# Elementwise work of a decoder layer's mixer, rebuilt: which engine does which step, and on how many columns

## The chip, the core and the metric

One core of a Trainium2 chip runs the whole kernel. The metric is device time in microseconds: three timed runs, of which the median counts. TensorE does the matmuls, VectorE (DVE), ScalarE (ACT) and GpSimd (POOL) the elementwise work, SyncE (SP) issues most DMAs. Each engine takes its instructions strictly in the order in which the kernel emits them, and waits for another engine by semaphores.

## What is computed

One inference step of one decoder layer, in float32, for 256 prompt tokens and 8 sample sequences of 8 tokens (320 columns; features lie on the partitions). Two head groups share one input projection:

```python
p = x @ w_in                                   # 2048 -> 5408
xc = causal_conv(u_x); r, i = sigmoid(xc @ wa + ba), sigmoid(xc @ wx + bx)
a = exp(-8 * r * softplus(-lam)); h_t = a_t * h_(t-1) + sqrt(1 - a*a) * (i * xc)     # RG-LRU, 8 blocks of 128
y_lru = h * gelu(u_gate)
z = u + (prev - u) * mu                        # RWKV-7: token shift of r, k, v and of three code tiles
w = exp(-exp(-0.5) * sigmoid(w0 + tanh(wd) @ w_up)); a = sigmoid(a0 + ad @ a_up); g = sigmoid(gd) @ g_up
kk = k * k_k; kk = kk / sqrt(max(sum(kk * kk), 1e-24)); k = k * (1 + (a - 1) * k_a)
S_t = S * w - (S kk) (kk * a)^T + v k^T; o_t = S_t r                                 # 16 heads of 64
y_rwkv = (group_norm(o) * ln_w + ln_b + sum(r * k * r_k) * v) * g
x = LN(ALPHA * x + [y_lru, y_rwkv] @ w_out); then cross-attention with its norm, then a squared-ReLU MLP with its norm
```

## The kernel before

**The main line** is a stream of 512 KB pieces of weights (`Stream`, lines 236 to 285). A piece is loaded on SyncE's queue, ScalarE rounds it to a first float32r part `wh`, and `Stream.poll` has the rest `wl = wraw - wh` made by VectorE or GpSimd. `mm_piece` (line 366) then runs three matmuls for each block of 128 x 128: `wh` with the two parts of the activations, and `wl` with the first. A feature tile of 128 rows and 320 columns takes 16 such blocks.

**The order** is made when the program is built. `Sched` (lines 108 to 208) keeps an estimated clock and an estimated free time of each engine (`account`), and side tasks are generators that it resumes between the stream's matmuls once their next step should be ready. `tt` (line 308) lets the engine with the earlier estimated end, VectorE or GpSimd, do a product or a sum of two tiles; `copy` chooses likewise between VectorE and ScalarE. Nothing of this is decided on the chip.

**The stages.** `w_in` (86 pieces) runs from the start to 516 us of the profile and `wk` (32 pieces, the memory keys, 256 columns) to 665 us; the mixer's side tasks run in these two, and `sch.drain()` at the end of `wk` finishes them. After it come `wv`, `w_out` with a layer norm, `wq`, attention, `wo` with a norm, and the MLP. `on_win` (line 1001) takes each finished tile of `w_in`: code tiles, then for each of 8 pairs of heads r, k, v, then x and gate of one LRU block.

**The side tasks** of the mixer, with the names that matter:

- `shifted` (539): ScalarE copies the tile from PSUM in two pieces, the difference to the token before is made by `tt`, then VectorE adds it in two `scalar_tensor_tensor` steps (256 columns, and 64 in sequences of 8). `sh_out` is kept by two GpSimd copies.
- `rwkv` (606): decays and keys; the norm of the keys is a matmul with the block of ones `bones` and a reciprocal over 320 columns; `BK` and `AR` (scaled b and k, a and r) are made in halves; their products inside the chunks become `GM`; then the sequence of four prompt chunks (729 to 763), where a chunk multiplies the state `S`, the inverse `XT` and the updates `UV`; at last the group norm, whose two sums are float32r matmuls of two parts of the tile (`halves`, `head_sums`) with a reciprocal over 320 columns.
- `invert` (797): the triangular inverses of the chunks. The products go to DRAM and back so that forty 16 x 16 blocks lie one to a partition (`Mp`, `Xp`); 30 dependent VectorE steps of 15 to 64 elements solve them (820 to 827); SyncE stores the result (828) and reads it back (833); then two levels of block products.
- `sample` (880): the 8 sample sequences as one more chunk.
- `lru_task` (934): convolution, the two gates (one as 1 / (1 + exp), the other as tanh of half), a scan, and the gate by tanh.

All matmuls of the side tasks but `head_sums` are plain float32, which the profile shows as two records each. An instruction that the planner accounts has line 230 (the wrapper), so groups are told apart by tiles. In a matmul's names the moving operand stands before the weights.

Of the kernel before, what the change touches and what calls it, by code (L numbers as in the profile page):

```python
# [9 lines left out]
F32 = mybir.dt.float32  # L10
F32R = mybir.dt.float32r
# [20 lines left out]
T_CODE = [24, 25, 26]                    # shift-tile numbers of the low-rank codes  # L32
WIN_TILES = []                           # (kind, index)
# [21 lines left out]
# constant block: identity, ones per 64-block, ones, room, masks  # L55
C_ID, C_BO, C_ONE, C_SEL, C_MU = 0, 128, 256, 384, 384 + 320
C_BM = C_MU + 256
C_MB = C_BM + 8
C_N = C_MB + 64


def _const_block():
# [12 lines left out]
    off = (t[:, None] // 32 == t[None, :] // 32) & (t[:, None] // 16 < t[None, :] // 16)  # L75
    c[:, C_MB:C_MB + 64] = np.tile(off, (2, 1))
# [3 lines left out]
# per-feature vectors: one column per 128-feature tile  # L80
# [9 lines left out]
# derived on chip  # L90
DER = {}
_n = 0
for _name, _w in (("w0h", 8), ("a0h", 8), ("ka2", 8), ("ka1", 8), ("nba", 8), ("bxh", 8), ("sp8", 8), ("nsp8", 8),
                  ("t0", 8), ("t1", 8), ("t2", 8), ("t3", 8), ("eps", 1), ("geps", 1), ("mdec", 1), ("pdec", 1)):
    DER[_name] = _n
    _n += _w
# [3 lines left out]
NTMP = 20           # temporaries of the mixer  # L100
NPB = 3             # pairs of heads in flight
# [5 lines left out]

class Sched:
    """Emission order for in-order engines: the weight stream is the main line; side tasks are generators that are
    resumed between its matmuls once what their next step needs should be there. A task yields before each step:  # L110
    PE if the step begins on the tensor engine, V, A or G to wait until that engine has little queued, a number of
    microseconds to wait."""

    def __init__(self):
        self.clock = 0.0
        self.free = {"V": 0.0, "A": 0.0, "G": 0.0}
        self.tasks = []
        self.cur = None
        self.poll = lambda: None

    def account(self, e, op, a, k):
# [4 lines left out]
        if e == "T":  # L126
            m = a[1].shape[-1]
            if a[1].dtype == F32R:
                c = max(n / 2400.0, 0.107)
            else:  # L130
                c = max(m / 128 * 0.214, 4 * n / 2400.0)
                c *= 0.3 if m <= 32 else 0.75 if m <= 64 else 1.0
            self.clock += c
            if self.cur is not None:
                self.cur.t = max(self.cur.t, self.clock + 0.2)
            return
        if e == "V":
            c = 0.06 + 5.5e-3 * n if op == "reciprocal" else 0.12 + 1.06e-3 * n
        elif e == "A":
            c = 0.22 + 0.75e-3 * n  # L140
# [8 lines left out]
    def pick(self, n, costs):  # L149
        """The engine that would be done first with n columns."""  # L150
# [10 lines left out]
    def run(self, gen, name=None):  # L161
        """A task whose first step comes at once."""
# [39 lines left out]
    def drain(self, upto=None, until=None):  # L202
        """Finish the tasks (up to and including the named one, or until something holds)."""
# [15 lines left out]
class Eng:  # L219
    """An engine whose instructions are accounted to the schedule."""  # L220
# [15 lines left out]
class Stream:  # L236
    """Weight pieces [128, 1024] in order of use: load, then the exact split into two float32r parts."""
# [11 lines left out]
    def poll(self, upto=None):  # L249
        """The second parts whose first parts should be there (up to piece upto: in any case)."""  # L250
# [37 lines left out]
def body(ctx, tc, I, O):  # L288
# [11 lines left out]

    def copy(out, in_):
        """From PSUM."""
        if sch.pick(cols(out), {"V": (0.12, 1.06e-3), "A": (0.22, 0.75e-3)}) == "V":
# [20 lines left out]
    # ---------------------------------------------------------------- constants  # L324
    K = cst.tile([128, C_N], F32, name="K")
# [3 lines left out]
    bones = K[:, C_BO:C_BO + 128]  # L329
    ones = K[:, C_ONE:C_ONE + 128]  # L330
    MU = K[:, C_MU:C_MU + 256].rearrange("p (c a t) -> p c a t", c=2, a=2)     # prompt chunks, sample chunk
    BM = K[:, C_BM:C_BM + 8]
    MB = K[:, C_MB:C_MB + 64]

# [10 lines left out]
    # ---------------------------------------------------------------- weight stream  # L345
# [20 lines left out]
    def mm_piece(i, p, g, act, N, ps, after=None):  # L366
        """Piece p of a group of g column tiles."""
# [16 lines left out]
    def mm_group(first, g, act, N, after=None):  # L384
        """One group of g 128-column tiles; returns their PSUM tiles."""
# [57 lines left out]
    Yraw = [unit(8 + i, dt=F32) for i in range(4)]      # mixer output, feature tiles 0-7 LRU, 8-15 RWKV  # L443
# [1199 lines left out]
```

## Time and profile before

| | |
|---|---|
| median of 3 runs (lowest, highest) | 2097.48 us (2093.6, 2099.22) |
| span of the profiled execution, first to last instruction | 2091.2 us |
| busy in the span: TensorE, VectorE, ScalarE, GpSimd | 97%, 57%, 42%, 30% |
| the first 665 us: VectorE, ScalarE, GpSimd busy | 516, 322, 342 us |
| the same: matmul records, idle time of TensorE | 5524, 39 us |
| mean granted TensorE clock, whole span | 0.984 of full speed |

The page gives no time of its own for the profiled execution beyond the span; the median run is 6.3 us longer than that span. Busy times of TensorE come from matmul records whose ends are modelled, so a stretch in which it is always busy need not be at its best rate. The time of a stage is read from what its bounding engine waits for there, and shares over the whole span mix stages with different limits.

### The profile page before, as it was taken

How to read it: one execution, taken by the hardware profiler on the slowest of the kernel's cores; microseconds unless marked ns; L12 is line 12 of the kernel's file. 1: busy time of each engine (PE TensorE's matmuls, PEld its weight loads, DVE VectorE, ACT ScalarE, POOL GpSimd, SP SyncE). 2: the span in 40 equal slices, each digit the busy share in tenths (PEclk: the TensorE clock that was granted, in tenths of full speed). 3: DMA queues.
4: the chain of work that ended last, by engine and by line, in shares of the span. 5: the costliest groups of instructions: out<-in, count | busy, mean ns of one | idle time of the engine just before them, and what ended most of it. 6: DMA issues, size and time to landing. Idle time of an engine off the chain costs nothing.

```text
span 2091.2 us, 37148 instructions
## 1 busy us (share of the span) xinstructions
PE 2029.5 (97%) x15142; PEld 1914.0 (92%) x15142; DVE 1185.7 (57%) x1764; ACT 888.0 (42%) x1430; POOL 636.8 (30%) x773
## 2 busy tenths in 40 slices
PE   8989999999999999999999999999999999999996
PEld 8978888888789899988899899999999999999996
DVE  6888788887855444644456644444444444434444
ACT  4534455455444433644433633233333333333333
POOL 4545565466634244621216610000000000000133
PEclk9989999899999999999999999999999999999998
DMA  7432323334346776578854454444454445555442
GB/s 240 137 112 84 109 85 112 99 102 137 124 153 209 240 250 193 181 276 300 310 170 145 126 152 148 150 149 152 152 151 148 147 152 150 151 152 148 146 151 91
DMA packets 120554, 333.60 MB, mean 160 GB/s; under 512 B 33040, under 2 KB 42288, under 8 KB 120384
## 3 DMA queue, kind: packets, MB, share of 16 engines
q1 hardware_dynamic: 105248, 279.46, 43.5%
q0 software_dynamic: 15136, 51.77, 6.9%
q8 instruction: 118, 1.93, 0.4%
q14 instruction: 52, 0.43, 0.1%
HBM read 315.53 MB, written 15.65 MB: 158 GB/s over the span
## 4 chain that ended last, share of the span: by engine, by line
PE 80%; DVE 11%; POOL 4%; issue 2%; DMA 1%; ACT 1%; POOLq 0%; ACTq 0%; DVEq 0%
PE ps L230 80%; DVE t L230 6%; DVE Xp L230 1%; POOL wl L230 1%; POOL t L230 1%; DVE u L230 1%; DVE BK L230 1%; DVE tt L230 1%; DVE wl L230 1%; DVE AR L230 1%; POOL u L230 1%; ACT wh L230 0%; POOL Mb L230 0%; DMA wraw<-in_w_in 0%; DMA kv<-mk 0%
## 5 line engine op out<-in xcount | busy, mean ns | idle before, releaser
L230 DVE TENSOR_TENSOR wl<-wraw,wh 128x1024 fp32r<-128x1024 f32 x435 | 552.5, 1271 | 557.8 <-ACT wh L230 557.1
L230 ACT CAST wh<-wraw 128x1024 fp32r<-128x1024 f32 x502 | 526.7, 1049 | 664.3 <-PE ps L230 592.7
L230 PE MATMUL ps<-u,wh 128*128 128x320 f32 (+1 forms) x3424 | 773.1, 316 | 9.4 <-ACT u L230 6.8
L230 PE MATMUL ps<-r,wh 128*128 128x320 f32 x3072 | 680.3, 310 | 2.3 <-ACT r L230 1.8
L230 PEld LDWEIGHTS ps<-u,wh 128*128 128x128 f32 x3424 | 574.6, 192 | 28.7 <-ACT u L230 6.8
L230 PE MATMUL ps<-u,wl 128*128 128x320 f32 (+1 forms) x1712 | 529.2, 309 | 8.0 <-DVE wl L230 5.2
L230 PEld LDWEIGHTS ps<-r,wh 128*128 128x128 f32 x3072 | 513.8, 188 | 10.6 <-issue 7.5
L230 PE MATMUL ps<-r,wl 128*128 128x320 f32 x1536 | 475.2, 309 | 0.6 <-POOL wl L230 0.6
L230 PEld LDWEIGHTS ps<-u,wl 128*128 128x128 f32 x1712 | 328.5, 192 | 9.1 <-DVE wl L230 5.7
L230 PEld LDWEIGHTS ps<-r,wl 128*128 128x128 f32 x1536 | 288.9, 188 | 0.8 <-POOL wl L230 0.8
L230 POOL TENSOR_TENSOR r<-r 128x320 f32<-128x320 f32 x64 | 46.1, 722 | 722.5 <-ACT r L230 722.5
L230 PE MATMUL ps<-h,wh 128*128 128x320 f32 x1024 | 225.6, 309 | 0.0
L230 POOL TENSOR_TENSOR wl<-wraw,wh 128x1024 fp32r<-128x1024 f32 x67 | 164.1, 2454 | 111.2 <-ACT wh L230 62.5
L230 PEld LDWEIGHTS ps<-h,wh 128*128 128x128 f32 x1024 | 171.4, 188 | 0.2
L230 PE MATMUL ps<-h,wl 128*128 128x320 f32 x512 | 158.2, 309 | 0.0
L230 DVE TENSOR_TENSOR u<-u,ps 128x320 f32<-128x320 f32 x134 | 61.7, 484 | 76.5 <-PE ps L230 73.8
L230 DVE SCALAR_TENSOR_TENSOR t<-t,W 128x256 f32<-128x256 f32 (+3 forms) x102 | 90.2, 913 | 17.0 <-POOL t L230 15.6
L230 PEld LDWEIGHTS ps<-h,wl 128*128 128x128 f32 x512 | 96.1, 188 | 0.0
L230 ACT ACTIVATE r<-ps 128x320 f32<-128x320 f32 x64 | 28.0, 438 | 157.6 <-PE ps L230 157.6
L230 POOL TENSOR_TENSOR s<-s,u 128x320 f32<-128x320 f32 x42 | 65.3, 1554 | 88.6 <-DVE u L230 88.3
L230 PE MATMUL ps<-wh,u 128*128 128x512 f32 x256 | 79.8, 391 | 0.0
L230 POOL TENSOR_TENSOR t<-t 128x320 f32<-128x320 f32 (+2 forms) x50 | 46.8, 936 | 88.0 <-DVE t L230 75.5
(235 smaller groups left out, 1873.1 us busy)
## 6 DMA issues: line engine op xcount, KB each, us to landing
wraw<-in_w SPq DMA_DIRECT2D x256, 512.0 KB, 3.6
wraw<-in_w_in SPq DMA_DIRECT2D x86, 512.0 KB, 4.5
wraw<-in_wk SPq DMA_DIRECT2D x32, 512.0 KB, 4.2
wraw<-in_wv SPq DMA_DIRECT2D x32, 512.0 KB, 4.3
wraw<-in_w_out SPq DMA_DIRECT2D x32, 512.0 KB, 4.2
kv<-in_cache_k POOLq DMA_DIRECT2D x32, 512.0 KB, 7.0
wraw<-in_wq SPq DMA_DIRECT2D x32, 512.0 KB, 4.7
kv<-in_cache_v POOLq DMA_DIRECT2D x32, 512.0 KB, 7.8
```

The source lines that it names most:

```text
L230: r = f(*a, **k)
```

## The change

It touches the mixer's side tasks and the planner's costs; the weights, the stages and the later math are the same. In words:

- **Planner.** New costs in `account`, among them a table switch of ScalarE (1.3) and a longer float32r matmul; while the mixer lasts, `tt` adds 6 us to GpSimd's estimate, so that VectorE gets nearly all of its steps, the parts `wl` among them.
- **Shift** straight from PSUM: one ScalarE pass by (1 - mu), a ScalarE copy for `sh_out`, and three VectorE steps, two of them with one operand in PSUM.
- **Norms** on a quarter of the columns: the sums of four quarters of 80 columns are laid on four groups of 32 partitions, square root and reciprocal run on 80 columns, and four matmuls with 0/1 blocks spread them again. The group norm's mean is taken by one float32 matmul with a centering block.
- **Gates** of the LRU by ScalarE's sigmoid, which takes away an addition and a reciprocal over 320 columns; a first tap of the convolution, state scaling and small output copies go from GpSimd to ScalarE.
- **BK** in one VectorE step; b and k of a head lie in the same rows, and the 64 x 128 matmuls become pairs of 64 x 64.
- **Heads alternated**: matmuls of the two heads that lie on different rows and columns of the array stand next to each other.
- **invert**: the 30 steps go from VectorE to GpSimd; the first block level handles half as many columns.

```diff
@@ Sched.account
-                c = max(n / 2400.0, 0.107)
+                c = (n + 32) / 2400.0
...
-            c = 0.06 + 5.5e-3 * n if op == "reciprocal" else 0.12 + 1.06e-3 * n
+            c = (0.06 + 6.5e-3 * n if op == "reciprocal" else 0.12 + 2.3e-3 * n if op == "tensor_tensor_scan" else
+                 0.15 + 1.05e-3 * n)
...
+            f = TABLE.get(a[2]) if op == "activation" else None
+            if f is not None:
+                if self.table not in f:
+                    self.table = f[0]
+                    c += 1.3
         else:
             c = 0.15 + 2.1e-3 * n
@@ tt
+    pool_wait = [6.0]
...
-        e = sch.pick(cols(out), {"V": (0.12, 1.06e-3), "G": (0.15, 2.1e-3)})
+        e = sch.pick(cols(out), {"V": (0.15, 1.05e-3), "G": (0.15 + pool_wait[0], 2.3e-3)})
@@ shifted
-            A.copy(ue[:, 1:257], ps[:, :NP])
-            A.copy(us[:, :, 1:9], ps[:, NP:NTOK].rearrange("p (b t) -> p b t", t=8))
...
-            tt(dd[:, 0:328], ue[:, 0:328], ue[:, 1:329], sub)
-            G.tensor_copy(sh_out[:, j, 0:1], ue[:, 256:257])
...
+            A.activation(out, ps[:, :NTOK], AF.Identity, scale=omu[:, j:j + 1])
+            A.copy(sh_out[:, j, :], ps[:, 255:NTOK:8])
+            V.scalar_tensor_tensor(out[:, 1:NP], ps[:, 0:NP - 1], vec("mu", j), out[:, 1:NP], op0=mult, op1=add)
+            V.scalar_tensor_tensor(seqs(out)[:, :, 1:8], seqs(ps)[:, :, 0:7], vec("mu", j), seqs(out)[:, :, 1:8],
+                                   op0=mult, op1=add)
+            V.tensor_add(out[:, NP:NTOK:8], out[:, NP:NTOK:8], shm[:, j, :])
@@ head_sums, head_spread
-            T.matmul(ps[:, :NTOK], bones_r, hl[0], start=True, stop=False)
-            T.matmul(ps[:, :NTOK], bones_r, hl[1], start=False, stop=True)
+            for j in range(4):
+                mm(ps[32 * j:32 * j + 32, 0:TB], bones[:, 48:80], x[:, TB * j:TB * j + TB])
+            return ps[:, 0:TB]
...
+            for j in range(4):
+                mm(ps[:, TB * j:TB * j + TB], K[:, C_SEL + 128 * j:C_SEL + 128 * j + 128], x)
+            return ps[:, :NTOK]
@@ rwkv
-            pn = ax()
-            T.matmul(pn[:, :NTOK], bones, k2, start=True, stop=True)
+            pn = head_sums(k2)
...
+            G.memset(P[:, 0:1], 1.0)
+            V.tensor_tensor_scan(P[:, 1:], d0, d1, 0.0, op0=mult, op1=add)
...
+            V.reciprocal(qn, qn)
...
+            pq = head_spread(qn)
...
-            for i, h in enumerate(HS):
-                tt(BK[h, :, 1 - i, :], c5(kk[h]), c5(Pi[h]), mult)
-                tt(BK[h, :, i, :], c5(km[h]), c5(Pi[h]), mult)
+            V.tensor_tensor(BK.rearrange("p c a t -> p a c t"), X2.rearrange("p a (c t) -> p a c t", t=64),
+                            c5(Pi).unsqueeze(1).to_broadcast([128, 2, 5, 64]), op=mult)
...
+            for c in range(4):
+                for s in range(2):
+                    for i, h in enumerate(HS):
+                        o, a = slots(i)[s]
+                        mm(pg[i][o, c * 128:c * 128 + 128], BK[h, c, a, :], AR[h, c, :, :])
...
+                if c:
+                    for i, h in enumerate(HS):
+                        mm(pr[HS[1 - i], 0:64], AR[h, c, 0, :], S[h, :], True, False)
                 for i, h in enumerate(HS):
...
-                    G.tensor_scalar(ts_, S, PT[:, c:c + 1], None, op0=mult)
+                    A.mul(ts_, S, PT[:, c:c + 1])
...
+                if c:
+                    for h in HS:
+                        mm(po[h, c * 64:c * 64 + 64], S[h, :], AR[h, c, 1, :], True, False)
                 for i, h in enumerate(HS):
-                    if c:
-                        mm(q, S[h, :], AR[h, c, 1, :], True, False)
-                    mm(q, UV[:, c, i, :], GM[:, i, c, 1, :], not c, True)
+                    mm(po[h, c * 64:c * 64 + 64], UV[:, c, i, :], GM[:, i, c, 1, :], not c, True)
...
-            o2 = halves(o)
...
-            V.reciprocal(q, q)
+            T.matmul(pc[:, :NTOK], CEN, o, start=True, stop=True)
...
+            pvr = head_sums(q)
...
+            V.reciprocal(qn, qn)
+            yield PE
+            pq = head_spread(qn)
@@ invert
-                V.tensor_tensor(o, Mp[:, j + 1:, j:j + 1].to_broadcast([40, r, w]),
+                G.tensor_tensor(o, Mp[:, j + 1:, j:j + 1].to_broadcast([40, r, w]),
                                 Xp[:, j:j + 1, 0:w].to_broadcast([40, r, w]), op=mult)
-                V.tensor_tensor(Xp[:, j + 1:, 0:w], Xp[:, j + 1:, 0:w], o, op=add)
+                G.tensor_tensor(Xp[:, j + 1:, 0:w], Xp[:, j + 1:, 0:w], o, op=add)
@@ lru_task
-            G.tensor_scalar(cv, ue[:, 0:344], vec("cw0", i), vec("cb", i), op0=mult, op1=add)
+            A.activation(cv, ue[:, 0:344], AF.Identity, scale=vec("cw0", i), bias=vec("cb", i))
...
-            A.activation(r, pa[:, :NTOK], AF.Exp, scale=-1.0, bias=der("nba", i))
-            A.activation(ti, px[:, :NTOK], AF.Tanh, scale=0.5, bias=der("bxh", i))
+            A.activation(r, pa[:, :NTOK], AF.Sigmoid, bias=vec("ba", i))
+            A.activation(ti, px[:, :NTOK], AF.Sigmoid, bias=vec("bx", i))
...
-            V.tensor_scalar(r, r, 1.0, None, op0=add)
-            V.reciprocal(r, r)
@@ after wk
         sch.drain()
+        pool_wait[0] = 0.0
```

## Rows read from the trace of the kernel before

**Rows 1.** Stretches: us, each engine's busy us (x instructions), granted clock, DMA share, GB/s.

```profile
0.00:516.00 516.00, 485.26 (x4144) 426.37 (x4145) 413.44 (x790) 257.58 (x503) 273.17 (x368) 0.96 0.39 121
516.00:665.00 149.00, 140.69 (x1380) 125.47 (x1379) 103.07 (x147) 64.12 (x114) 68.88 (x79) 0.97 0.50 157
845.00:1166.00 321.00, 317.18 (x2347) 289.72 (x2342) 175.51 (x272) 146.03 (x269) 109.33 (x121) 1.00 0.66 225
```

**Rows 2.** TensorE timeline at the end of wk: start us, us, engine, instruction.

```profile
645.91 1.24 PE L230 MATMUL ps<-sg,lg 128*128 128x320 f32 x4
```

**Rows 3.** Waits of TensorE in 0:665: us in total, times, longest.

```profile
PE ps L230 <- ACT u L230: 6.8, 1, 6.8
```

**Rows 4.** VectorE timeline, 107 to 114 us.

```profile
107.36 2.35 DVE L230 TENSOR_TENSOR Xp<-Xp,tt 40x64 f32<-40x64 f32 x1
110.66 3.36 DVE L230 TENSOR_TENSOR wl<-wraw,wh 128x1024 fp32r<-128x1024 f32 x1
```

**Rows 5.** GpSimd timeline, the same stretch.

```profile
107.23 2.40 POOL L230 TENSOR_TENSOR wl<-wraw,wh 128x1024 fp32r<-128x1024 f32 x1
```

**Rows 6.** TensorE timeline, the same stretch; in brackets the idle time before.

```profile
114.07 0.41 PE L230 MATMUL ps<-u,wl 128*128 128x320 f32 x1 [4.28 <-DVE wl L230]
```

**Rows 7.** Stretches, columns as in rows 1: either side of a change of clock.

```profile
142.00:152.00 10.00, 10.00 (x53) 9.14 (x54) 5.91 (x16) 1.91 (x6) 4.60 (x12) 0.50 0.38 84
153.00:163.00 10.00, 10.00 (x114) 8.79 (x111) 5.91 (x17) 5.62 (x15) 4.34 (x7) 1.00 0.46 159
```

**Rows 8.** VectorE groups in 0:665: xcount | busy us, mean ns | idle before.

```profile
L230 DVE TENSOR_TENSOR wl<-wraw,wh 128x1024 fp32r<-128x1024 f32 x63 | 85.6, 1362 | 24.5 <-ACT wh L230 24.4
L230 DVE RECIPROCAL t<-t 128x320 f32<-128x320 f32 x32 | 68.5, 2139 | 0.3
L230 DVE SCALAR_TENSOR_TENSOR t<-t,W 128x64 f32<-128x64 f32 x35 | 46.2, 1320 | 0.0
L230 DVE TENSOR_TENSOR BK<-t 64x320 f32<-64x320 f32 x32 | 21.6, 714 | 0.7
L230 DVE SCALAR_TENSOR_TENSOR S<-ps,PT,ts 128x64 f32<-128x64 f32 x24 | 6.7, 278 | 5.0 <-PE ps L230 3.8 <-POOL Xp L817 1.0
```

**Rows 9.** All of one tile, VectorE: xcount: ns min/median/max, first to last start.

```profile
L230 DVE TENSOR_TENSOR Xp<-Xp,tt x120: 166/201/2350, 99.0 to 577.2; 40x15 f32<-40x15 f32 x16, 40x28 f32<-40x28 f32 x16, 40x39 f32<-40x39 f32 x16, 40x48 f32<-40x48 f32 x16
```

**Rows 10.** GpSimd groups in 0:665, columns as in rows 8.

```profile
L230 POOL TENSOR_TENSOR wl<-wraw,wh 128x1024 fp32r<-128x1024 f32 x57 | 139.8, 2456 | 55.0 <-ACT wh L230 46.4 <-PE ps L230 8.2
L982 POOL COPY h_out<-t 128x1 f32<-128x1 f32 x8 | 5.1, 632 | 22.4 <-DVE t L230 22.4
```

**Rows 11.** ScalarE timeline around a table load.

```profile
225.19 1.28 ACT L230 ACT_TABLE_LOAD   x1
226.48 0.47 ACT L230 ACTIVATE t<-t 128x320 f32<-128x320 f32 x1
```

**Rows 12.** TensorE timeline: start us, us, instruction, xrecords merged; six places.

```profile
106.16 0.70 PE L230 MATMUL ps<-t,K 128*128 128x320 f32 x2
...
196.52 1.71 PE L230 MATMUL ps<-AR,BK 64*128 64x128 f32 x16 [0.22 <-DVE AR L230]
...
264.79 0.45 PE L230 MATMUL ps<-t,bones_r 128*128 128x320 f32 x2
...
295.40 0.34 PE L230 MATMUL ps<-UV,BT 128*64 128x64 f32 x4
295.66 0.33 PE L230 MATMUL ps<-AR,S 64*64 64x64 f32 x2
295.92 0.33 PE L230 MATMUL ps<-GM,UV 128*64 128x64 f32 x2
...
301.52 0.34 PE L230 MATMUL ps<-S,AR 64*64 64x64 f32 x4
...
848.00 1.01 PE L230 MATMUL ps<-cb,K 128*128 128x80 f32 x8
```

**Rows 13.** SyncE's queue, all of the span: waited for, us in total, times, longest.

```profile
SPq L828 <- DVE Xp L230: 85.0, 7, 22.4
```

More of the change, by code (lines that the diff above doesn't have):

```diff
@@ L53 @@
 G_WO = [(0, 4), (4, 2)] + [(m, 1) for m in range(6, 16)]
-C_ID, C_BO, C_ONE, C_SEL, C_MU = 0, 128, 256, 384, 384 + 320
+C_ID, C_ONE, C_SEL, C_BO = 0, 128, 256, 256 + 512
+C_MU = C_BO + 128
 C_BM = C_MU + 256
-C_MB = C_BM + 8
-C_N = C_MB + 64
+C_CEN = C_BM + 8
+C_ODD = C_CEN + 128
+C_N = C_ODD + 1
 def _const_block():
@@ L97 @@
 NDER = _n
-NTMP = 20
+NTMP = 18
 NPB = 3
@@ L118, in __init__ @@
         self.cur = None
+        self.table = 0
         self.poll = lambda: None
@@ L457, in derive @@
         V.memset(der("mdec"), -0.5 * DECAY)
-        V.memset(der("pdec"), 0.5 * DECAY)
         yield
@@ L520, in body @@
         sg = p1.tile([128, 2, NTOK], F32, name="sg")
+        d0 = p1.tile([128, NTOK], F32, name="d0")
         d1 = p1.tile([128, NTOK], F32, name="d1")
+        nc.gpsimd.memset(d0, 0.0)
         nc.gpsimd.memset(d1, 0.0)
@@ L681, in rwkv @@
             UV4 = pp.tile([128, 2, 64], F32, name="UV4")
-            p4 = []
+            p4 = [ax(), ax()]
+            for s in range(2):
+                for i, h in enumerate(HS):
+                    o, a = slots(i)[s]
+                    mm(p4[i][o, 0:128], BK[h, 4, a, :], AR[h, 4, :, :])
+            for s in range(2):
+                for i, h in enumerate(HS):
+                    o, a = slots(i)[s]
+                    mm(p4[i][o, 128:192], BK[h, 4, a, :], ident[h, h])
             for i, h in enumerate(HS):
-                p4.append(ax())
-                mm(p4[i][:, 0:128], BK[h, 4, :, :], AR[h, 4, :, :])
-                mm(p4[i][:, 128:192], BK[h, 4, :, :], ident[h, h])
                 mm(p4[i][h, 192:256], zv[h, 256:320], ident[h, h])
@@ L704, in rwkv @@
             UV = p2.tile([128, 4, 2, 64], F32, name="UV")
-            pt = ax()
+            pt = [ax(), ax()]
             for c in range(4):
-                mm(pt[:, c * 128:c * 128 + 128], both(BK[:, c]), ident)
+                for s in range(2):
+                    for i, h in enumerate(HS):
+                        o, a = slots(i)[s]
+                        mm(pt[i][o, c * 64:c * 64 + 64], BK[h, c, a, :], ident[h, h])
             yield
-            copy(BT, pt.rearrange("p (c x) -> p c x", c=4))
+            for i in range(2):
+                copy(BT[:, :, 64 * i:64 * i + 64], pt[i][:, :256].rearrange("p (c x) -> p c x", c=4))
             yield PE
@@ L812, in invert @@
             sch.dma()
-            Mb = p1.tile([128, 5, 64], F32, name="Mb")
-            for h in range(2):
-                o = HS[1 - h]
-                G.tensor_tensor(Mb[o], GM[o, h, :, 0, :], MB[o, None, :].to_broadcast([64, 5, 64]), op=mult)
             nc.gpsimd.memset(Xp, 0.0)
@@ L893, in sample @@
                 mm(pr[HS[1 - i], 0:64], RO[h, 0, :], ident[h, h], True, False)
+            for i, h in enumerate(HS):
                 mm(pr[HS[1 - i], 0:64], GM[h, i, 4, 0, :], UV[h, i, :], False, True)
@@ L910, in sample @@
             for i, h in enumerate(HS):
-                o = po[h, 0:64]
-                mm(o, UV[:, i, :], GM[:, i, 4, 1, :], True, False)
-                mm(o, ident[h, h], RO[h, 1, :], False, True)
+                mm(po[h, 0:64], UV[:, i, :], GM[:, i, 4, 1, :], True, False)
+            for h in HS:
+                mm(po[h, 0:64], ident[h, h], RO[h, 1, :], False, True)
             res["po"] = po
@@ L1008, in on_win @@
                 t = tmp()
-                g = shifted({"r": 0, "k": 8, "v": 16}[kind] + i, ps, t)
-                if m < 4:
-                    sch.run(g, "codes")
-                else:
-                    for _ in g:
-                        pass
+                shifted({"r": 0, "k": 8, "v": 16}[kind] + i, ps, t)
                 z[kind, i] = t
```

207 lines of the change are left out of this document (92 added, 115 removed).

## The prediction, made before the changed kernel ran

> **What bounds the kernel now.** I read the page first (TensorE 97% busy), then the stretches by stage, then what TensorE waits for in the mixer, then one stall on three engines, then the groups of VectorE and GpSimd. The mixer is the first 665 us. There TensorE is idle 30.7 + 8.3 = 39 us, against 3.8 us in the 321 us of attention [rows 1], where side tasks also run; 6.8 us of the 39 are the first load [rows 3], so 32 us are stalls. The granted clock averages 0.96 and 0.97 in the mixer and 1.00 in attention [rows 1]. Its two levels are 2.4 and 1.2 GHz: at 0.50 ten microseconds held 53 matmul records, right after at 1.00 they held 114 [rows 7]. So (0.04 x 516 + 0.03 x 149) x 2 = 50 us ran at 1.2 GHz and lost about 25. Stalls and clock together are 57 us, and they hang together: the fall to 0.50 at 142 us follows a stall.
>
> Why the stalls? VectorE is busy 413 + 103 = 516 of 665 us [rows 1] and works in order, so the part `wl` that the stream needs stands behind side work. Much of that busy time is waiting inside instructions. At 107.23 GpSimd begins a split of 2.40 us [rows 5]; VectorE's 64-element step issued at 107.36 takes 2.35 us, and a split at 110.66 takes 3.36 [rows 4], while that small step's median is 0.20 [rows 9]. TensorE, waiting for that split, stands 4.28 us [rows 6]. The same in the groups: the shift's second step (64 columns, operands in SBUF) means 1320 ns, a step of 64 columns with one operand in PSUM 278 [rows 8]. A VectorE step with two SBUF tensors and a GpSimd one exclude each other, and GpSimd's are long: 57 splits of 2456 ns [rows 10].
>
> **The change, part by part.**
>
> *VectorE.* Waiting in the shift's 35 short steps goes: 35 x (1320 - 278) = 36 us [rows 8]. The 240 substitution steps leave: 240 x 0.20 = 48 us, taking the products like the sums [rows 9]. Of 32 reciprocals 24 leave and 16 of a quarter width come, by columns 535 ns each: 51 - 9 = 42 us [rows 8]. BK: 32 half steps of 714 ns become 8 of twice the columns, 23 - 11 = 12 us [rows 8]. In come the 57 splits, at the present mean of 1362 ns 78 us [rows 8], and some 50 smaller steps from GpSimd, at 0.5 us 25 us. So 516 - 138 + 103 = 481 us at most, an upper bound, since those means still hold waiting. If the waiting in the other groups goes as it does in the shift, 400. I take 420, of a shorter mixer of about 615 us: 68% instead of 78%, and no step of it held for 2 us.
>
> *Stalls and clock.* Attention shows what is left when the side work fits: 1.2% idle at VectorE 55%, ScalarE 45% and GpSimd 34% [rows 1]. The mixer will be fuller than that, so I leave a quarter of the 57 us: **-43 us**. Bounds: -57 (all goes) and -20 (the waits move to another engine).
>
> *TensorE's own work.* In the chunk's output matmuls each head's two now run one after the other, 0.26 us from start to start (295.66, 295.92), four in a step; four records of one kind on two heads, `UV,BT`, take the same 0.26 us together (295.40 to 295.66) [rows 12]. Alternated, the step takes two such times instead of four: 0.52 us less, 24 prompt steps and 8 sample ones, **-16 us**. The first products of a chunk gain nothing: there the four records of `S,AR` of both heads already stand together [rows 12], although the program alternates the kinds.
> By the Trainium skill, page TensorE: Matmul & The Clock Gate, section Part 3: Packing small matmuls, matmuls keep program order strictly in start and end. The `S,AR` record contradicts that; by the page those 24 steps would gain another 0.26 us each, 6 us, and the sum would be 2042.
> The norms cost: today a key norm is one float32 matmul of 320 columns (0.70 us) and a group norm two pairs of 0.45 [rows 12]. After, each pair of heads has two spreads, each at most the 1.01 us of the same shape in the layer norm, two sets of quarter sums, at most as long, and a centering matmul of 0.70 [rows 12]. Durations overlap, so I take half the quarter sums and 0.9 for a spread: 1.0 + 1.8 + 0.7 - 1.6 = 1.9 us, less the pipelined ends about 1.5: 8 x 1.5 = **+12 us**, bounds +7 and +20. The 64 x 128 products (1.71 us for 16 records [rows 12]) become twice as many half as wide: the same if pairs overlap like `UV,BT`, 8 x 1.7 = 14 us more if they don't; I take **-2 us**, with the small blocks of `invert`. Together -6, from -18 to +20.
>
> *ScalarE* gains the convolution's tap, state scaling, small copies (some 90 steps of 0.2 to 0.6 us, less the two roundings per norm) and table switches: the sigmoid stands between functions of other tables, up to 2 more switches per LRU block, 16 x 1.28 = 20 us [rows 11]. 322 + 36 us of 615 is 58%: costs nothing while no queue forms before the casts `wh`; if the cover goes, it is the -20 above.
> By the Trainium skill, page ScalarE: Activation LUTs, section What ACT_TABLE_LOAD costs, a switch has another 1.38 us of draining behind the load. Here the next instruction starts 0.01 us after it [rows 11]; by the page ScalarE would get 22 us more, and I would give the partial rival below 0.30 instead of 0.20.
>
> *Moved waits.* The substitution now runs in GpSimd's queue. Behind it wait a memset in front of each pair's scan (so VectorE's queue, the splits in it and TensorE), the chunk ends `PT`, and in `wk` the stores of the keys, whose issue waits for ScalarE. SyncE's store of `Xp` waits for it too, with weight loads behind; that wait is already 85 us in 7 times [rows 13]. A step costs from VectorE's 0.20 [rows 9] to GpSimd's 0.63 for a contended step of one element [rows 10]; I take 0.35, nearer the first, since uncontended: 10 us a pair, which the three pairs in flight hide. The planner counts 30 x 0.15 + 1360 x 0.0021 = 7.4 us.
>
> *The tail.* The last pair's gate runs at 645.9 [rows 2], 19 us before `wk` ends; `wk` shrinks by its idle 8.3 and clock loss 4.5, which the cover holds.
>
> The later stages get other planner costs only, and TensorE bounds them: 0, within 5 us.
>
> Sum: 2091.2 - 43 - 16 + 12 - 2 = 2042 of span; the median run lies 6.3 us above the profiled span, so **2048 us**.
>
> **The rivals.**
>
> *Partial:* ScalarE, or GpSimd as far as the planner still gives it splits (its 6 us give way when VectorE's queue is longer), holds the stream instead. For it: ScalarE gets as full as VectorE is in attention; every split now hangs on one engine. Against: its longest steps are 1.3 us. With -20 for the stalls and -6 for the matmuls: 2072.
>
> *More:* every stall goes, and the alternation also pays in the other products: -57 - 18: 2022.
>
> *None:* the change doesn't free VectorE (481 us of a 610 us mixer is 79%, as before) and the norms' matmuls eat the alternation: 2097, within 0.3%.
>
> *Slower:* the substitution on GpSimd comes later than the planner believes; VectorE's transposes, emitted by its clock, stand at the head of VectorE's queue, and the store of `Xp` holds the weight loads. It decides from about 0.6 us a step (18 us for a chain, 11 more than planned, where two pieces of prefetch, at 615 / 118 = 5.2 us a piece, cover 10). At 0.75 us a chain takes 22 us: 5 us beyond the cover, and as much on the transposes and for the clock after it, 8 x 10 = 80 us against 49 gained: 2097 + 31 = 2128. For it: steps of 0.63 exist [rows 10]. Against: GpSimd will have little else to do, and VectorE's steps that exclude it are mostly 0.5 us.
>
> **How the numbers follow.** Forecast (2025 to 2062) 0.58, partial (2062 to 2091) 0.20, more (below 2025) 0.08, none 0.05, slower 0.09. The range that should hold 8 in 10: from the "more" case, 2022, to the partial case with the norms' upper bound, 2085. About 0.3% (6 us) is what this kernel's measurement can tell from no change: faster by more 0.86, within 0.05, slower 0.09.
>
> **What would show it.** Right: TensorE idle in the mixer near 15 us and its clock near 0.99 there; the shift's short step near 0.28 us; no splits on GpSimd before 620 us; `AR,S` records of both heads together; the mixer's end near 615. Wrong: GpSimd's substitution steps above 0.6 us, weight loads or VectorE's transposes at the end of TensorE's waits, ScalarE's casts late, or a mixer that is no shorter although VectorE is freer.

## The result, and the profile after

The changed kernel took 2047.6 us (median of four runs, 2044.3 to 2050.6) against 2098.4 before, also four: a ratio of 0.9767, 95% interval 0.975 to 0.9783. The forecast was 2048.

The profile is of the slowest of the four, 2050.6 us with a span of 2048.5. Stretches of the kernel after, columns as in [rows 1]: the stream of the input projection (now to 473 us), the memory keys (to 614), and attention with the matmuls around it (795 to 1119, in before 845 to 1166).

```profile
0.00:473.00 473.00, 455.14 (x4735) 399.79 (x4736) 308.93 (x649) 264.90 (x532) 106.92 (x293) 0.99 0.42 132
473.00:614.00 141.00, 136.59 (x1397) 122.51 (x1396) 74.79 (x126) 59.63 (x107) 33.14 (x70) 0.96 0.53 166
795.00:1119.00 324.00, 317.80 (x2338) 289.42 (x2336) 179.34 (x271) 145.39 (x268) 106.76 (x121) 1.00 0.64 223
```

The mixer ends at 613.6 us instead of 664.6. VectorE is busy 384 of 614 us instead of 516 of 665, GpSimd 140 instead of 342, and the granted clock is 0.99 and 0.96 instead of 0.96 and 0.97 [rows 1]. What TensorE waits for in that time:

```profile
PE ps L246 <- DVE wl L246: 8.8, 7, 2.5
PE ps L246 <- ACT u L246: 6.6, 1, 6.6
PE ps L246 <- DMA Xn<-bx: 2.0, 1, 2.0
PE ps L246 <- DVE UV L246: 1.8, 3, 0.7
```

The first load (6.6) is as before [rows 3]; the rest adds up to some 16 us, and no single wait is as long as the 4.28 of [rows 6]. In the kernel before, these were among the longest:

```profile
PE ps L230 <- POOL t L230: 5.3, 2, 2.6
PE ps L230 <- DVE S L230: 4.6, 3, 1.8
PE ps L230 <- DVE t L230: 4.4, 4, 1.8
PE ps L230 <- DVE wl L230: 4.3, 1, 4.3
```

Of the 32 us before, 21.6 end on VectorE and 10.7 on GpSimd (`t`, `wl`, `u`). The 4.28 us that the prediction shows is the only wait there for a `wl` of VectorE's; most of the others are for tiles of the side tasks. After, none of the waits ends on GpSimd. VectorE's and GpSimd's groups up to 614 us, columns as in [rows 8]:

```profile
L246 DVE TENSOR_TENSOR wl<-wraw,wh 128x1024 fp32r<-128x1024 f32 x118 | 145.9, 1240 | 40.9 <-ACT wh L246 40.8
L246 DVE RECIPROCAL t<-t 128x320 f32<-128x320 f32 x8 | 17.2, 2145 | 0.0
...
L246 DVE SCALAR_TENSOR_TENSOR t<-ps,W,t 128x56 f32<-128x56 f32 x27 | 7.2, 266 | 0.0
...
L246 DVE TENSOR_TENSOR BK<-X,t 128x640 f32<-128x640 f32 x8 | 6.6, 825 | 0.3
...
L246 DVE RECIPROCAL qn<-qn 128x80 f32<-128x80 f32 x8 | 5.1, 636 | 5.4 <-ACT qn L246 5.4
...
L246 POOL TENSOR_TENSOR wl<-wraw,wh 128x1024 fp32r<-128x1024 f32 x2 | 5.6, 2793 | 6.3 <-ACT wh L246 6.3
```

118 splits run on VectorE where there were 63, and their mean fell from 1362 to 1240 ns [rows 8]. The shift's short step fell from 1320 to 266 ns, a reciprocal of 80 columns takes 640, one of 320 still 2145. GpSimd kept 2 splits of 57 [rows 10]. Its substitution, and SyncE's wait for it (columns as in [rows 9] and [rows 13]):

```profile
L246 POOL TENSOR_TENSOR Xp<-Xp,tt x120: 211/292/1354, 89.9 to 519.7; 40x15 f32<-40x15 f32 x16, 40x28 f32<-40x28 f32 x16, 40x39 f32<-40x39 f32 x16, 40x48 f32<-40x48 f32 x16
...
SPq L855 <- POOL Xp L246: 86.4, 6, 17.0
```

The product steps (202/281/1320) are like these. All 240 together take 92.6 us, 0.39 a step. TensorE in a chunk's outputs, then a spread and the quarter sums of a norm:

```profile
217.38 0.34 PE L246 MATMUL ps<-UV,BT 128*64 128x64 f32 x4
217.64 0.33 PE L246 MATMUL ps<-AR,S 64*64 64x64 f32 x4
217.91 0.34 PE L246 MATMUL ps<-GM,UV 128*64 128x64 f32 x4
...
208.48 1.12 PE L246 MATMUL ps<-qg,K 128*128 128x80 f32 x8
...
220.67 0.34 PE L246 MATMUL ps<-t,KM 128*32 128x80 f32 x8
```

`AR,S` now stands with the four records of both heads together, then `GM,UV`; each lot takes 0.27 us from start to start. Before, they came two by two [rows 12].

One of the stalls that are left (GpSimd, VectorE, TensorE, then the stretches beside the clock change):

```profile
159.20 2.38 POOL L246 TENSOR_TENSOR wl<-wraw,wh 128x1024 fp32r<-128x1024 f32 x1 [3.21 <-ACT wh L246]
...
159.26 3.39 DVE L246 TENSOR_TENSOR wl<-wraw,wh 128x1024 fp32r<-128x1024 f32 x1
...
162.71 0.63 PE L246 MATMUL ps<-u,wl 128*128 128x320 f32 x1 [2.51 <-DVE wl L246]
...
162.30:165.60 3.30, 2.89 (x10) 2.63 (x10) 0.35 (x1) 0.00 (x0) 0.90 (x4) 0.50 0.51 170
166.00:169.30 3.30, 3.30 (x60) 3.03 (x60) 2.90 (x8) 0.75 (x3) 0.00 (x0) 1.00 0.51 177
```

The planner found VectorE's queue more than 6 us behind and gave GpSimd a split. VectorE's own split, begun 0.06 us later, took 3.39 us instead of 1.2, TensorE stood 2.51 us, and from 162.3 to 165.7 us the clock was 0.50. The stall at 359 us, also followed by 3.4 us at 0.50, is of another kind (VectorE, then TensorE):

```profile
359.77 0.67 DVE L246 SCALAR_TENSOR_TENSOR t<-ps,W,t 128x255 f32<-128x255 f32 x2 [6.13 <-ACT sh_out L246]
360.43 1.22 DVE L246 TENSOR_TENSOR wl<-wraw,wh 128x1024 fp32r<-128x1024 f32 x1
...
361.70 0.42 PE L246 MATMUL ps<-u,wl 128*128 128x320 f32 x1 [2.29 <-DVE wl L246]
```

No GpSimd step ran there, and VectorE had stood idle for 6.13 us. At the head of its queue was the new shift, which waits for TensorE's tile and ScalarE's pass over it, and the split stood behind it. So a queue is late by its order too, and not only by its work. The longest stretch at 0.50 (527.5 to 537.7 us, 10.2 of the mixer's 17.1) came where TensorE waited 1.99 us for the inverse's blocks to come back from DRAM (`Xn<-bx`).

Four numbers for the mixer serve for all kernels below. They come from the TensorE records between the first stream matmul and the first of `wv`. *Idle* is the sum of the gaps between them. *Side* is the time from start to start of all matmuls that aren't the stream's (each at most 0.7 us, so it holds short waits and slow clock too). *Slow* is the time at 1.2 GHz, half of which is lost. *End* is the start of `wv`. *Change* is the ratio's distance from 1 times 2096 us; an interval is about 3 to 4 us to either side of it. The other columns are of one execution each: the runs of the kernel before alone had granted clocks from 0.978 to 0.985 over the span, which is some 29 us of slow time from one end to the other, so small differences in that column mean nothing.

| kernel | ratio (95%) | change | idle | side | slow | end |
|---|---|---|---|---|---|---|
| before | 1 | | 32.3 | 181.1 | 51.2 | 664.6 |
| after | 0.9767 (0.975-0.9783) | -49 | 15.6 | 155.5 | 17.1 | 613.6 |
| before, bias alone | 1.0077 (1.0064-1.009) | +16 | 46.6 | 198.9 | 88.7 | 678.3 |
| before, substitution on GpSimd alone | 0.9891 (0.9876-0.9906) | -23 | 19.7 | 179.4 | 37.5 | 639.7 |
| before, shift from PSUM alone | 0.9883 (0.9865-0.9901) | -25 | 22.3 | 173.8 | 30.7 | 639.2 |
| before, sigmoids alone | 0.9879 (0.9863-0.9894) | -25 | 20.4 | 172.9 | 30.7 | 638.8 |
| before, matmuls alone | 0.9952 (0.9934-0.9969) | -10 | 54.5 | 148.4 | 44.4 | 647.5 |
| after, no bias | 0.9762 (0.9744-0.9781) | -50 | 14.2 | 147.8 | 13.7 | 606.5 |
| after, substitution on VectorE | 0.9865 (0.9849-0.9881) | -28 | 28.1 | 162.3 | 51.2 | 636.6 |
| after, heads in series | 0.9809 (0.9794-0.9825) | -40 | 12.0 | 168.0 | 3.4 | 620.9 |
| after, full-width norms | 0.9738 (0.9724-0.9751) | -55 | 17.2 | 148.7 | 20.5 | 603.1 |
| after, planner's old costs | 0.9696 (0.9678-0.9714) | -64 | 11.3 | 146.5 | 10.2 | 598.7 |
| after, old TensorE costs | 0.9736 (0.9723-0.975) | -55 | 17.0 | 152.5 | 17.1 | 610.1 |
| after, old costs and full-width norms | 0.9759 (0.9743-0.9775) | -51 | 27.6 | 136.0 | 23.9 | 615.6 |

### The profile page after: what moved, and what is told of

The parts are those of the page before. It is cut to its first block, busy times and chain, and to the rows that moved or that the text cites. A ratio compares the mean times of both kernels' runs of the same rounds, so it can differ in the third digit from the quotient of the medians.

```text
span 2048.5 us, 38116 instructions
## 1 busy us (share of the span) xinstructions
PE 1999.3 (98%) x15750; PEld 1887.1 (92%) x15750; DVE 1054.7 (51%) x1604; ACT 890.8 (43%) x1452; POOL 430.3 (21%) x689
## 4 chain that ended last, share of the span: by engine, by line
PE 90%; DVE 3%; POOL 3%; issue 1%; DMA 1%; ACT 1%; SPq 0%; POOLq 0%; ACTq 0%; DVEq 0%
PE ps L246 90%; DVE wl L246 1%; DVE t L246 1%; POOL wl L246 1%; DVE u L246 1%; POOL tt L246 1%; POOL u L246 0%; POOL Xp L246 0%; ACT wh L246 0%; POOL r L246 0%; DMA t<-in_x 0%; DMA Xn<-bx 0%; DMA kv<-in_cache_k 0%; ACT u L246 0%; DMA Mp<-bm 0%
## 5 line engine op out<-in xcount | busy, mean ns | idle before, releaser
L246 DVE TENSOR_TENSOR wl<-wraw,wh 128x1024 fp32r<-128x1024 f32 x490 | 616.0, 1259 | 579.5 <-ACT wh L246 578.8
L246 PE MATMUL ps<-u,wh 128*128 128x320 f32 (+1 forms) x3424 | 764.0, 313 | 7.5 <-ACT u L246 6.6
L246 PEld LDWEIGHTS ps<-u,wh 128*128 128x128 f32 x3424 | 566.5, 190 | 27.9 <-issue 7.7
L246 POOL TENSOR_TENSOR tt<-Mp,Xp 40x15 f32<-40x15 f32 (+7 forms) x120 | 46.8, 390 | 191.8 <-DMA Mp<-bm 183.5
L246 PEld LDWEIGHTS ps<-wh,u 128*128 128x128 f32 x256 | 48.1, 188 | 10.1
```

What stands on the lines that cost most here:

```text
L246: r = f(*a, **k)
```

## The experiments

**Are GpSimd's long steps the cause of the stalls?** The prediction said so. The bias that takes the splits from GpSimd was removed from the changed kernel, and put alone into the kernel before.

```diff
-    pool_wait = [6.0]
+    pool_wait = [0.0]
```

> The changed kernel with its 6 us bias against GpSimd set to 0 in the mixer; all else as changed. Theory (GpSimd's long steps hold VectorE's steps that have two SBUF tensors): some 50 to 60 of the 118 splits go back to GpSimd, VectorE's two-SBUF steps beside them take 1 to 3 us, while the shift's short step, which reads PSUM, stays near its 266 ns; TensorE's idle time in the mixer goes from 16 us back to about 30, its time at 1.2 GHz from 17 to about 45 us, and the kernel takes about 2048 + 25 = 2073 us. Rival (the planner's new costs alone keep the queues short, so it does not matter where the splits run): splits return, but idle and clock stay, 2044 to 2052 us.

25 splits went back to GpSimd (27 there instead of 2), and the time did not move: 2048.3 us, -50 against -49. GpSimd's and VectorE's groups, up to 614 us:

```profile
L246 POOL TENSOR_TENSOR wl<-wraw,wh 128x1024 fp32r<-128x1024 f32 x27 | 65.3, 2421 | 150.6 <-ACT wh L246 150.6
...
L246 DVE TENSOR_TENSOR wl<-wraw,wh 128x1024 fp32r<-128x1024 f32 x94 | 115.3, 1230 | 45.6 <-ACT wh L246 45.1
...
L246 DVE SCALAR_TENSOR_TENSOR t<-ps,W,t 128x56 f32<-128x56 f32 x27 | 7.2, 267 | 0.0
```

The shift's step from PSUM stayed at 267 ns, so that part of the theory held. That the splits' place set the time did not: summed over VectorE's groups up to 614 us, the time above each group's 10th percentile rose from 14 to 35 us, without effect. Only 25 came back, not the 50 to 60 of the expectation, so how the kernel would run with all of them there is not shown; the planner leaves VectorE only when it believes it late.

```diff
-        e = sch.pick(cols(out), {"V": (0.12, 1.06e-3), "G": (0.15, 2.1e-3)})
+        e = sch.pick(cols(out), {"V": (0.12, 1.06e-3), "G": (0.15 + pool_wait[0], 2.1e-3)})
```

> The kernel before with one part of the change alone: the planner's choice between VectorE and GpSimd gets the 6 us against GpSimd in the mixer, so most of the 57 splits and the shift's differences go to VectorE. Theory A (the stalls come from how much work, above all the dependent substitution steps, stands in VectorE's queue ahead of the splits): 57 x 1.36 = 78 us more on an engine that is busy 516 of 665 us; no gain or a loss, 2090 to 2125 us. Theory B (they come from GpSimd's 2.4 us steps, which hold VectorE's steps with two SBUF tensors): the long waits inside VectorE's small steps go, and with them 20 to 40 us of stalls and slow clock, 2055 to 2077 us.

Slower by 16 us, as theory A had it. The mixer as a stretch, two VectorE groups in it, and two waits of TensorE:

```profile
0.00:678.00 678.00, 624.53 (x5519) 553.62 (x5520) 501.13 (x1025) 325.94 (x627) 190.07 (x342) 0.93 0.41 126
...
L230 DVE TENSOR_TENSOR wl<-wraw,wh 128x1024 fp32r<-128x1024 f32 x101 | 128.4, 1273 | 36.3 <-ACT wh L230 36.2
...
L230 DVE SCALAR_TENSOR_TENSOR t<-t,W 128x64 f32<-128x64 f32 x35 | 16.6, 475 | 0.0
...
PE ps L230 <- DVE wl L230: 7.3, 5, 2.0
PE ps L230 <- DVE tt L230: 5.5, 1, 5.5
```

The mutual exclusion is real: with 101 splits on VectorE, the shift's short step fell from 1320 to 475 ns [rows 8]. The same sum over VectorE's groups fell from 132 to 53 us. But VectorE is busy 501 us, nearly the old 516: the splits took the place of the waits. Idle rose from 32 to 47 us, and the time at 1.2 GHz from 51 to 89. The splits now stand in the queue of the 240 substitution steps; the longest wait (5.5 us) and two of the five for `wl` have such steps shortly ahead in VectorE's queue. That this is what the 16 us are is the reading that fits; no run with the bias and the substitution on GpSimd alone tests it.

**Which part relieves VectorE's queue?** First the substitution, both ways.

```diff
-                G.tensor_tensor(o, Mp[:, j + 1:, j:j + 1].to_broadcast([40, r, w]),
+                V.tensor_tensor(o, Mp[:, j + 1:, j:j + 1].to_broadcast([40, r, w]),
...
-                G.tensor_tensor(Xp[:, j + 1:, 0:w], Xp[:, j + 1:, 0:w], o, op=add)
+                V.tensor_tensor(Xp[:, j + 1:, 0:w], Xp[:, j + 1:, 0:w], o, op=add)
```

> The changed kernel with the 240 substitution steps back on VectorE. Theory (VectorE's fullness makes the stalls, GpSimd's chain is covered by three pairs in flight): VectorE gets 240 x 0.20 = 48 us more, 70% of the mixer instead of 62.5%; TensorE's idle time grows by 3 to 8 us, and with the clock the kernel takes 2051 to 2062 us. Rival (the chain on GpSimd, 0.39 us a step instead of 0.20, is what TensorE's transposes and SyncE's stores wait for): 11.5 us less GpSimd time per pair goes into the path of the inverses, 2038 to 2046 us.

> The kernel before with one part of the change alone: the 240 substitution steps run on GpSimd. Theory A (VectorE's queue): 48 us less on VectorE; the 20 us that putting them back cost the changed kernel come off here, 2070 to 2082 us. Rival (the slower case of the prediction: GpSimd, which here still has 57 splits of 2.46 us, hands the inverses over late): steps stand behind splits, a pair's chain takes 20 us or more instead of 6, TensorE and the stores wait for it, 2100 to 2130 us.

Back on VectorE it cost 20 us, more than the 3 to 14 expected; moved alone in the kernel before, it saved 23. The changed kernel with the substitution on VectorE, its mixer and two waits of TensorE:

```profile
0.00:636.00 636.00, 600.83 (x6123) 531.59 (x6124) 420.04 (x978) 331.70 (x668) 49.07 (x128) 0.96 0.43 135
...
PE ps L246 <- DVE wl L246: 14.5, 7, 4.3
...
PE ps L246 <- DVE S L246: 3.0, 2, 1.9
```

VectorE is busy 420 of 636 us, 66%, less than before (78%), and yet the slow time is the whole 51.2 us again, and idle 28.1 is nearly the old 32.3. So the busy share alone does not order these kernels. TensorE waits for `wl` 14.5 us instead of 8.8, with 118 splits on VectorE as in the changed kernel. Only one of those waits (2.8 us) has a substitution chain shortly ahead in VectorE's queue; two (4.6 us) stand behind a shift for which VectorE waited 3.7 and 5.6 us idle. So how the added steps came to delay the splits is not shown beyond that they stand in the same queue. The rival, that GpSimd hands the inverses over late, fell in both kernels, also where GpSimd still ran 40 splits.

Two other parts alone, in the kernel before: the token shift read from PSUM (`shifted` as in the change's diff), and the two gates as sigmoids.

```diff
-            A.activation(r, pa[:, :NTOK], AF.Exp, scale=-1.0, bias=der("nba", i))
+            A.activation(r, pa[:, :NTOK], AF.Sigmoid, bias=vec("ba", i))
...
-            V.tensor_scalar(r, r, 1.0, None, op0=add)
-            V.reciprocal(r, r)
```

> The kernel before with the token shift read from PSUM alone. It takes the 328-column differences from VectorE and GpSimd and the waits from the 35 short steps, 36 us of VectorE's time. Theory A (whatever fills VectorE's queue costs, waits included; 48 us of substitution were worth 20 to 23): 2078 to 2088 us. Rival (waits for GpSimd inside VectorE's steps cost nothing, as the bias alone, which removed such waits, brought no gain): 2092 to 2098 us.

> The kernel before with the LRU's two gates as sigmoids alone: 8 reciprocals of 2.14 us and 8 additions less on VectorE, some 20 us; up to 16 more table loads of 1.28 us on ScalarE. Theory A (VectorE's queue, 20 us per 48): 2085 to 2092 us. Rival (the table loads delay ScalarE's casts by as much): 2093 to 2105 us.

Each saved 25 us, more than theory A's best (18 and 11), and the rivals fell. In all three single parts idle fell from 32 to 20-22 us and the slow time from 51 to 31-38 (for the substitution, 37.5, within what executions of one kernel differ by). Fewer waits inside VectorE's steps are not the reason: with the shift alone and with the sigmoids alone, the sum above the 10th percentiles is still 117 us of 132.

These prices must be read with care. 23 + 25 + 25 + 10 for the matmuls is 83 us, and all together brought 49; but the change also holds parts that cost, the bias (16 alone) and, as shown below, the norms (6) and the new costs (15), and 83 - 16 - 6 - 15 is 46. So these sums don't show whether the parts share their stalls, and no run with two of them tests it. Each part also reshuffles the planner's order, and new costs, which change only that and the choice of engines, turn out below to be worth 15 us. The substitution, 20 and 23 us in two different kernels, is the firmest price.

**What is TensorE's own time worth?** The matmuls alone in the kernel before, and the heads in series in the changed one:

```diff
-                for c in range(4):
-                    mm(pg[i][:, c * 128:c * 128 + 128], both(BK[h, c]), AR[h, c, :, :])
+            for c in range(4):
+                for s in range(2):
+                    for i, h in enumerate(HS):
+                        mm(pg[i][HS[s], c * 128:c * 128 + 128], BK[h, c, s, :], AR[h, c, :, :])
```

> The kernel before with the change's matmuls alone: chunk outputs with the heads alternated, and the products with BK as twice as many of 64 columns instead of 128. By the times from start to start, the outputs save 15 us of TensorE and the BK products 16 (the serial order showed that the latter come from the form, not from the order). Theory (TensorE's own work is on the path through the whole mixer, beside VectorE's stalls): most of the 31 us, 2066 to 2078 us. Rival (the mixer is set by VectorE's queue, and time won on TensorE is waited out there): 2084 to 2097 us.

```diff
-                if c:
-                    for h in HS:
-                        mm(po[h, c * 64:c * 64 + 64], S[h, :], AR[h, c, 1, :], True, False)
                 for i, h in enumerate(HS):
+                    if c:
+                        mm(po[h, c * 64:c * 64 + 64], S[h, :], AR[h, c, 1, :], True, False)
                     mm(po[h, c * 64:c * 64 + 64], UV[:, c, i, :], GM[:, i, c, 1, :], not c, True)
...
-                for s in range(2):
-                    for i, h in enumerate(HS):
+                for i, h in enumerate(HS):
+                    for s in range(2):
```

> The changed kernel with the matmuls of one pair's two heads emitted one head after the other again, in the chunk outputs (both prompt and sample) and in the four groups of 64 x 128 and 64 x 64 products with BK; same instructions, other order. Theory (matmuls of two heads overlap only when they stand next to each other): the chunk outputs cost 15 us more and the BK products 16 more, from the times from start to start of before and after; 2048 + 31 = 2079 us if all of it is on TensorE's path. Rival 1 (the price stated beforehand): 16 + 2, 2066 us. Rival 2 (the time disappears in gaps that TensorE has anyway): under 8 us, 2048 to 2056.

In the kernel before, side work fell by 33 us, near the 31 counted, but only 10 reached the time: idle rose from 32 to 54 us. The rival was right. (The edit also copies the transposed `BK` out in two pieces instead of one.) Its mixer, and what TensorE then waited for:

```profile
0.00:647.00 647.00, 585.81 (x5901) 515.42 (x5902) 518.31 (x944) 319.42 (x617) 332.84 (x443) 0.97 0.42 132
...
PE ps L230 <- DVE t L230: 22.7, 12, 6.0
PE ps L230 <- DVE S L230: 13.1, 8, 3.4
```

TensorE caught up with VectorE: 22.7 us for the elementwise tiles `t`, where it had been 4.4, and 13.1 for the state `S` instead of 4.6. In the changed kernel, where VectorE has room, the series added 15 us of output matmuls and cost 9, near rival 2's bound of 8; idle fell from 15.6 to 12.0 us meanwhile and slow time from 17.1 to 3.4, so it seems that a part of the 15 went where TensorE had lost time. An output step there, columns as in [rows 12]:

```profile
220.47 0.33 PE L246 MATMUL ps<-AR,S 64*64 64x64 f32 x2
220.72 0.33 PE L246 MATMUL ps<-GM,UV 128*64 128x64 f32 x2
220.98 0.32 PE L246 MATMUL ps<-AR,S 64*64 64x64 f32 x2
221.24 0.33 PE L246 MATMUL ps<-GM,UV 128*64 128x64 f32 x2
```

That is the pattern of before [rows 12]. By form and from start to start, the outputs (`AR,S`, `GM,UV`, `RO,K`) take 34.6 us in the mixer before, 19.4 after and 34.1 in series. The products with `BK` take 32.9, 16.9 and 16.0: their gain is the same in either order. It comes with their being 64 x 64 instead of 128 columns wide. My expectation of 16 us more for their order was wrong.

**What do the norms and the planner's costs do?**

```diff
-            for j in range(4):
-                mm(ps[32 * j:32 * j + 32, 0:TB], bones[:, 48:80], x[:, TB * j:TB * j + TB])
-            return ps[:, 0:TB]
+            mm(ps[:, :NTOK], bones, x)
+            return ps[:, :NTOK]
...
-            pq = head_spread(qn)
+            pq = qn
```

> The changed kernel with the key norm and the group norm's variance at full width again: one float32 matmul of 320 columns for the sums instead of four quarter sums and four spreads, the root and the reciprocal over 320 columns. TensorE: the quarter sums and spreads took 4.4 + 7.0 + 7.2 = 18.6 us from start to start; 16 matmuls of 320 columns at 0.49 us are 7.8, so 11 us less. VectorE: 16 reciprocals of 2.15 us instead of 0.64, 24 us more. Theory A (VectorE's load makes stalls, by the substitution 20 us for 48): -11 + 10, 2042 to 2052 us. Rival (VectorE has room for it; only TensorE's own work counts): 2034 to 2039 us.

```diff
-                c = (n + 32) / 2400.0
+                c = max(n / 2400.0, 0.107)
...
-            c = 0.2 + 0.85e-3 * n
+            c = 0.22 + 0.75e-3 * n
```

> The changed kernel with the planner's costs of before in the accounting and in the choice of engines; the 6 us bias against GpSimd and every instruction of the mixer's mathematics as changed. Theory (the costs only move places of emission): 2043 to 2055 us. Rival (the gain comes from the planner's better costs, which know table loads and the slower scan): TensorE's idle and slow clock in the mixer come back, some 33 us, 2075 to 2085 us. It also shows the later stages, whose only change are these costs: 1427 us before, 1435 in the profile after; theory 1430 to 1435 whichever costs.

> The changed kernel with the planner's costs of before for TensorE alone (a stream matmul of 320 columns counted at 0.133 us, where it takes 0.147; small float32 ones dearer); the new costs of VectorE and ScalarE (table loads, scan) stay. With all costs of before the changed kernel took 2031.6 us, 17 less than with the new ones. Theory T (a planner's clock that runs behind the chip resumes side work later than it could, which leaves slack on each queue): all of it comes from these two lines, 2029 to 2036 us. Rival (the new table loads and the dearer scan hold side tasks back, so they bunch up): the time stays at 2044 to 2050 us.

> The changed kernel with the planner's costs of before and the norms at full width: the two edits that were faster by 17 and by 6 us, together. Theory (they are independent): 2048 - 23 = 2025 us, 2021 to 2030. Rival (both gain from the same slack: the 24 us of reciprocals on VectorE stall the shorter mixer): 2030 to 2036 us.

Neither expectation had the result of the old costs: alone they made the changed kernel 15 us faster, 2031.6 us, the fastest of all; some 6 of it come with TensorE's costs alone (2040.8, between its two theories). (The edit also takes back the other new lines in `account`, `copy` and `tt`.) Full-width norms alone were 6 us faster, at the edge of what the intervals can tell, and 2041.8 us lies between their two theories. Both together should have given 2025 us and gave 2044, above both expectations: the second edit took back what the first had gained, and idle went from 11.3 to 27.6. A part of why is in two places of VectorE's timeline, with TensorE's after the first:

```profile
290.27 2.14 DVE L240 RECIPROCAL t<-t 128x320 f32<-128x320 f32 x1
292.45 0.82 DVE L240 TENSOR_TENSOR BK<-X,t 128x640 f32<-128x640 f32 x1
293.19 0.48 DVE L240 SCALAR_TENSOR_TENSOR AR<-t 128x320 f32<-128x320 f32 x1
293.60 0.48 DVE L240 TENSOR_TENSOR AR<-t 128x320 f32<-128x320 f32 x1
294.00 2.14 DVE L240 RECIPROCAL t<-t 128x320 f32<-128x320 f32 x1
296.06 1.16 DVE L240 TENSOR_TENSOR wl<-wraw,wh 128x1024 fp32r<-128x1024 f32 x1
...
297.27 0.64 PE L240 MATMUL ps<-u,wl 128*128 128x320 f32 x1 [3.10 <-DVE wl L240]
...
304.00 0.67 DVE L240 SCALAR_TENSOR_TENSOR t<-ps,W,t 128x255 f32<-128x255 f32 x2 [6.79 <-ACT sh_out L240]
```

With the old costs, the full-width reciprocal of one pair's group norm lands right behind the reciprocal and the products of another pair: 5.8 us of VectorE in one piece ahead of a split, and TensorE stands 3.10 us. The same pattern stands at 362 and 424 us; the three stalls make 7.7 us. Four others, 9.5 us together, are of the kind seen at 359 us in the changed kernel: at 304.00 VectorE has stood idle 6.79 us for a shift, with the split behind it. The kernel with the old costs alone has neither kind. So what a norm's width and the planner's costs are worth here hangs on which steps meet in the queue; a rule for it is not shown. How much of the 15 us another harmless reshuffle would bring or take is open.

## Why the prediction was right, and where its steps failed

**The sum.** The forecast of the span, 2042, is 6 under the profiled 2048.5, and 3 under that of the median runs (2045.4 and 2045.6). The mixer's end was put at 615 and came at 613.6.

That the sum came out is in part luck. By the two profiles, stalls and clock brought 9 us less than forecast, TensorE's own work some 14 more, and the later stages took 8 back.

**The step from span to median failed.** It added 6.3 us, as if every run lay so far above its span. The four runs after lie 2.1 us above their own spans. With that, the profiled execution of before (2091.2) belongs to its fastest run, 2093.6. The 4 us too much met a span that was forecast 3.5 too short. The later stages took 8 us more than before in this profile (1418.9 against 1410.5, from the first matmul of `wv` to TensorE's last), past the 5 allowed. The seven other kernels with all of the old costs took 1412 to 1416 there, and the five with all of the new ones 1416 to 1420: some 4 us go with the new costs, and the rest is most likely the difference between two executions.

**Stalls and clock: the size was nearly right, the cause half wrong.** Forecast -43; idle fell by 16.7 us and the slow time by 34.1, which is 17 lost: -34. That VectorE's queue carried the stalls held for two thirds of them (21.6 of 32 us before). That GpSimd's long steps were what filled it, so that taking the splits away would free it, did not: the exclusion exists, but alone its removal cost 16 us, and its return for 25 splits nothing. The failed step is the one that read "VectorE waits inside its instructions" as "waiting is the cause". A queue is as late behind a wait as behind work of the same length; the single parts that gained took work from VectorE (substitution, reciprocals, the differences of the shift). How far each of them did so by the order that it left is open. VectorE came out at 384 us where I took 420, for the waits went nearly everywhere: 14 us above the 10th percentiles.

**TensorE's own work: -6 forecast, about -20 by form.** The outputs were right (-15 against -16) and so were the norms: from 14.8 to 26.4 us (with the matmul of the bonus, the sum over r k, which stays), +12 as forecast. The -2 for the products with `BK` was -16, the mis-sized term; the question that I asked there (do pairs overlap or not) was the wrong one. The `S,AR` step gained nothing, as its record of before said (4.0 us before, 3.8 after). The 6 us that follow from the strict order of the Trainium skill's page TensorE: Matmul & The Clock Gate, section Part 3: Packing small matmuls, did not come; the trace decides.

**What was costed at nothing.** GpSimd's substitution came at 0.39 us a step, near the 0.35, and SyncE's longest wait for it is 17.0 instead of 22.4 [rows 13]: the slower rival didn't come. A trace of it did: the longest stretch of slow clock, 10.2 us, follows a wait for the inverse's way back. ScalarE is busy 325 us, not 358, with 8 more table loads, not 16. The planner's new costs were weighed for the later stages only; they gave 15 us away against the old ones, some 4 of them in those stages.

**The rivals.** "None" and "slower" fell. The partial case and "more" did not come.

## What to carry to other kernels

When an engine's instructions wait inside themselves, take work off its queue before shuffling the work that makes it wait; a bias that swaps waits for the same amount of work gained nothing here. Look also at what stands at the head of the queue: a split can be late behind an idle engine whose next step waits for another (2.29 us of TensorE at 359 us). Time won on an engine that is waiting for another's queue is waited out there: the same matmuls were worth 33 us of TensorE's time and 10 us of the kernel's. And a part's price alone is not its price in the whole: the bias cost 16 us in one kernel and nothing in the other, and two edits that gained 15 and 6 us gained 2 together. Where a planner deals out the order, some 15 us either way can be the order's and not the edit's.

## What the hardware showed that was not expected

Float32 products of 64 rows by 64 columns ran in half the time of the same work in tiles of 128 columns (16.9 against 32.9 us), in both orders of emission that were tried (16.0 in series); the chunk outputs, whose second product (128 by 64) takes all rows, did need the heads side by side (19.4 against 34.1).
At full clock, a stream matmul of 320 columns ahead of a matmul on a part of the array (fewer than 128 rows or columns) takes 0.239 us from start to start instead of 0.147; ahead of a float32 one of 128 by 128 it takes 0.148. The mixer after has 157 steps of the first kind, some 14 us by that estimate, so how the side work is clumped costs TensorE time of its own.
